# Scores in fewer groups: four blocks of a sliding pair at once, and blocks 2 and 3 of a differential head at once

## The chip, the cores and the metric

The kernel runs on one core of a Trainium2 chip. A core has five engines with queues of their own: TensorE (PE, with its weight loads shown apart as PEld), VectorE (DVE), ScalarE (ACT), GpSimd (POOL) and SyncE (SP), and it has DMA queues. The metric is the device time of one execution in microseconds, lower is better.

## The reference

One decoder layer over 512 tokens of width 1024, batch 1, in fp32. The part around the change is the attention; `h` is the normalised input.

```
qa, ka, va, qd, kd, vd, ga, gd = split(h @ w_in)
# A: sliding window of 128, 8 query heads on 2 key heads of width 64, blocks of 128 queries
scores = qa_block . [previous block, this block of ka] / 8 - slope * distance, outside: -1e30
out_a  = softmax([scores, sink])[..., :-1] @ [previous, this block of va]
# B: differential, 4 heads, each with two maps of width 64 and values of width 128, causal
p      = softmax(qd . kd / 8 - slope * distance), for the two maps
out_d  = rmsnorm((p[0] - lam * p[1]) @ vd) * (1 - 0.2)
merged = sigmoid(ga) * (out_a @ w_branch_swa) + sigmoid(gd) * (out_d @ w_branch_diff)
x      = x + gate1 * (merged @ w_out)
# then a gated MLP with a causal convolution of width 3, and a final norm
```

## The kernel before, in words

Every fp32 product is made from a high and a low part: three matmuls (high by high, high by low, low by high) that add up in one PSUM bank. `mm3` (lines 119 to 121) does so with all 128 rows of the array. In the attention `mm3_rows` (line 126) takes two products at once, each with a contraction of 64, one on rows 0 to 63 and one on rows 64 to 127: the three matmuls of both go out in turns, so that a block of scores for two heads (or two maps) is three pairs of matmuls.

TensorE's order in the attention is written out by hand (`manual_schedule` with TensorE alone): it executes exactly in the order of the program text. VectorE and ScalarE are put in order by a planner, which takes what is ready by its own estimate of time, with priority in the order of the program; operations under `high_priority` (the score reductions, the softmax, the copies of transposes) come before all others, and the rows of the modulation (`arow`, line 757) in part before the rest.

TensorE's gaps are filled with `fill(n)`: n steps, each of three full matmuls of 512 columns that belong to a projection (query, key and value of the differential heads: `pq`, `pk`, `pw`; the gates and branch products of the sliding part: `pga`, `pA`). `fill` also starts the loads of the weights ahead, and every eighth step one piece of the modulation.

The sliding part works on four pairs of heads, `i` = 0 to 3. `swa_scores(i, n0)` makes the scores of two blocks, n0 and n0 + 1, in two PSUM banks; VectorE adds the distances and takes the maxima (line 559, tile `st`). `swa_softmax` has ScalarE take the exponentials and VectorE scale them; `swa_transpose(i, j)` has TensorE transpose the probabilities of one head (line 593, seven transposes, tile `tp`), and ScalarE copies them; `swa_values(i)` (line 604) multiplies them by the values into a bank `oa`, which ScalarE and VectorE copy out (`outah` at line 430, `outal` at line 431). The loop over pairs has this order: scores of blocks 0 and 1 of pair i + 1, two steps, transposes of the first head of pair i, two steps, transposes of the second head, scores of blocks 2 and 3 of pair i + 1, two steps, softmax of pair i + 1, two steps, values of pair i, three steps.

The differential part goes over 16 blocks, s = 4h + n. `diff_scores` makes the scores of a block for two maps (tile `sd`), 128(n + 1) columns wide, and VectorE's reductions follow (line 673); blocks 0 and 1 share a pair of banks and are made together. `diff_softmax` follows, then `diff_transpose` (line 702, tile `td`) and, once a head is done, `diff_values` (tile `od`), whose bank ScalarE empties (lines 719 and 720). In a turn of the loop come two steps, the scores of later blocks, four steps, the transposes of block s, the softmax of the blocks just scored. In the turn of block 1 the scores of block 2 are made, in that of block 2 those of block 3, in that of block 3 those of blocks 0 and 1 of the next head. Some turns have norm sums (`pss`, line 725) or transposes of values (`pv`) between, at fixed counts of steps.

PSUM has eight banks. Here they go by tags: two `f` for projections, three `s` for scores, two `t` for transposes, and one `v` (`vbank`) for the values of both parts and, before, for a projection of the first stage. A tile of a tag waits until the tile before it in that bank has been read.

## Time and profile before

| | us |
|---|---|
| median of 3 runs | 706.9 (706.72 to 707.26) |
| profiled execution | 708.24 |
| span of its instructions | 705.4 |
| TensorE matmuls busy | 685.0 |
| VectorE busy | 578.4 |
| ScalarE busy | 383.9 |

The span is the time from the first to the last instruction; the execution has 2.84 us around it. The mean granted TensorE clock was 0.994 of full speed. Sliding attention lies from about 61 to 117 us, differential attention from 117 to 217 us. In rows in order of time, the first number is the start in us, the second the duration, then engine, line, operation, output and inputs, shapes and the count of instructions merged into the row, and in brackets the idle time before it and what ended it. A matmul's row lasts longer than the distance to the next start, as matmuls overlap.

### The profile page before, as it was taken

What the parts mean: (1) busy time and instruction counts of PE and PEld (TensorE: products, weight loads), DVE (VectorE), ACT (ScalarE), POOL (GpSimd) and SP (SyncE); (2) the same over time, 40 slices, a digit from 0 to 9 for tenths busy, and PEclk for the clock granted to TensorE, in tenths of its full rate; (3) what the DMA queues carried; (4) which work ended last, traced back from release to release, by engine and by line L of the source; (5) the groups of instructions that cost most, each with busy time, mean ns of one, the idle gap of its engine ahead of it and who ended that gap; (6) DMA issues with size and microseconds to landing.
All of it is one profiled execution on the core that took longest, in us unless ns stands there. A gap on an engine that the chain in (4) does not pass through costs nothing. (4 is left out here: it accounts for less than half of the span.)

```text
span 705.4 us, 11197 instructions
## 1 busy us (share of the span) xinstructions
PE 685.0 (97%) x4155; PEld 597.1 (85%) x4155; DVE 578.4 (82%) x1107; ACT 383.9 (54%) x676; POOL 82.2 (12%) x100
## 2 busy tenths in 40 slices
PE   6999999999999999999999999999999999999994
PEld 6777777777787888888889999999999999888884
DVE  5998968788985766773579899888888999979996
ACT  3646766545543333431468656555555666656664
POOL 3000000000011000000030111111101102530300
PEclk9999999999999999999999999999999999999998
DMA  9983624263543774529617888786979748996803
GB/s 311 302 262 98 201 61 154 67 199 90 170 153 100 262 214 142 186 93 288 187 33 148 197 199 204 177 209 182 208 204 230 164 143 204 197 200 191 158 0 119
DMA packets 115861, 121.80 MB, mean 173 GB/s; under 512 B 4415, under 2 KB 93280, under 8 KB 115808
## 3 DMA queue, kind: packets, MB, share of 16 engines
q1 hardware_dynamic: 96894, 95.09, 42.7%
q0 software_dynamic: 18720, 25.73, 21.6%
q8 instruction: 32, 0.52, 0.3%
q10 hardware_dynamic: 194, 0.28, 0.1%
q14 instruction: 21, 0.17, 0.1%
HBM read 118.97 MB, written 2.11 MB: 172 GB/s over the span
## 5 line engine op out<-in xcount | busy, mean ns | idle before, releaser
L1126 PE MATMUL up<-t,m_whi 128*128 128x256 f32 x528 | 96.1, 283 | 0.0
L1126 PEld LDWEIGHTS up<-t,m_whi 128*128 128x128 f32 x528 | 82.3, 192 | 0.0
L1126 PE MATMUL up<-t,m_wlo 128*128 128x256 f32 x264 | 74.7, 283 | 0.1
L1126 PE MATMUL up<-bh,p_wlo 128*128 128x256 f32 x232 | 65.7, 284 | 0.7 <-DVE p_wlo L1069 0.7
L1126 PE MATMUL up<-bh,p_whi 128*128 128x256 f32 x232 | 65.6, 283 | 0.0
L1126 PE MATMUL up<-bl,p_whi 128*128 128x256 f32 x232 | 65.6, 283 | 0.0
L1126 PEld LDWEIGHTS up<-t,m_wlo 128*128 128x128 f32 x264 | 50.6, 192 | 0.3 <-DVE m_wlo L1069 0.3
L1126 PEld LDWEIGHTS up<-bh,p_wlo 128*128 128x128 f32 x232 | 44.5, 192 | 1.1 <-DVE p_wlo L1069 1.1
L1126 PEld LDWEIGHTS up<-bh,p_whi 128*128 128x128 f32 x232 | 44.5, 192 | 0.0
L1126 PEld LDWEIGHTS up<-bl,p_whi 128*128 128x128 f32 x232 | 44.5, 192 | 0.0
L757 DVE SCALAR_TENSOR_TENSOR arow<-ra,cs,arow 128x512 f32<-128x512 f32 x56 | 41.9, 747 | 2.6 <-DMA ra<-in_w_ada_dram 1.8
L1037 POOL DMA_DIRECT2D s<-in_w_up_dram x21 | 27.0, 1361 | 142.9 <-DMA s<-in_w_up_dram 78.0
L1069 DVE TENSOR_TENSOR m_wlo<-s,m_whi 128x1024 fp32r<-128x1024 f32 x31 | 37.7, 1217 | 2.0 <-ACT m_whi L1065 2.0
L1065 ACT CAST m_whi<-s 128x1024 fp32r<-128x1024 f32 x31 | 32.5, 1047 | 9.4 <-DVE s L1059 5.9
L1126 PE MATMUL up<-t,p_whi 128*128 128x256 f32 x176 | 32.2, 283 | 0.0
L687 ACT ACTIVATE sd<-sd,dmx 128x128 f32<-128x128 f32 (+3 forms) x32 | 17.8, 556 | 23.2 <-DVE dmx L685 15.9
L175 POOL TENSOR_TENSOR r<-ms,mhalf 128x1 f32<-128x1 f32 (+1 forms) x16 | 13.2, 828 | 144.7 <-DVE ms L173 74.0
L1126 PEld LDWEIGHTS up<-t,p_whi 128*128 128x128 f32 x176 | 27.4, 192 | 0.2 <-issue 0.2
L1133 ACT ACTIVATE gT<-a,cv 128x512 f32<-128x512 f32 x22 | 17.7, 813 | 17.6 <-DVE a L1168 17.3
L770 POOL DMA_DIRECT2D mod_rows<-arow x8 | 4.3, 540 | 193.7 <-ACT arow L769 193.5
L1065 ACT CAST p_whi<-wa 128x1024 fp32r<-128x1024 f32 x18 | 18.7, 1041 | 12.0 <-PE up L1126 7.2
L1126 PE MATMUL up<-t,p_wlo 128*128 128x256 f32 x88 | 24.9, 283 | 0.0
(478 smaller groups left out, 2073.0 us busy)
## 6 DMA issues: line engine op xcount, KB each, us to landing
ra<-in_w_ada_dram SPq DMA_DIRECT2D x32, 512.0 KB, 4.2
wa<-in_w_up_dram SPq DMA_DIRECT2D x22, 512.0 KB, 4.6
s<-in_w_up_dram SPq DMA_DIRECT2D x21, 512.0 KB, 5.1
s<-in_w_up_dram POOLq DMA_DIRECT2D x21, 512.0 KB, 7.0
adaw<-in_w_ada_dram SPq DMA_DIRECT2D x16, 512.0 KB, 4.9
w<-in_w_in_dram SPq DMA_DIRECT2D x12, 512.0 KB, 4.1
a<-in_w_up_dram SPq DMA_DIRECT2D x11, 512.0 KB, 4.8
b<-in_w_down_dram SPq DMA_DIRECT2D x10, 512.0 KB, 4.7
```

The costliest lines, as they stand in the source:

```text
L175: nc.gpsimd.tensor_tensor(r0, ms, mhalf[:, :n], ALU.pow)
L687: nc.scalar.activation(pm[m], pm[m], AF.Exp, bias=mx[:, m : m + 1], scale=slope, accum_out=lsum[:, m : m + 1])
L757: nc.vector.scalar_tensor_tensor(ac, r[:, a], cc, ac, ALU.mult, ALU.add)
L770: nc.gpsimd.dma_start(mod_rows[idx : idx + 1, hf * S : (hf + 1) * S], row)
L1037: nc.gpsimd.dma_start(dst, upblock(*blk), accum_op=ALU.add)
L1065: nc.scalar.copy(W[J, name][0], R[J, SRC[name]])
L1069: nc.vector.tensor_sub(lo, R[J, SRC[name]], hi.bitcast(F32))
L1126: nc.tensor.matmul(o[u], w[:, k, cu], b[:, k], start=name in ("p1", "m5", "p2") and k == 0 and x == 0, stop=k == 3 and x == 2, skip_group_ ...
L1133: nc.scalar.activation(grow(j), av[J][:, u], AF.Identity, bias=cv[:, 66 + j : 67 + j], scale=cv[:, 44 + j : 45 + j])
```

## The change

`swa_scores` takes a list of blocks. Pair 0 keeps its two calls, (0, 1) and (2, 3). Pairs 1 to 3 have all four blocks made in one call, so that 24 matmuls of 64 rows follow each other; they write four banks, three of tag `s` and, for blocks 2 and 3 of the second head, the one of tag `v`. The call stands behind the first two steps of a turn, directly ahead of the transposes of the first head, and the second call behind the transposes of the second head is gone. All eight reductions of the pair follow the one call.

In the differential part the scores of block 2 and block 3 are made together in the turn of block 1; the turn of block 2 makes none. The second map of block 3 takes the bank of tag `v`. The number of matmuls, reductions and transposes is unchanged, as are the steps of `fill`.

```diff
-    def swa_scores(i, n0):
-        if n0 == 0:
+    def swa_scores(i, blocks):
+        if 0 in blocks:
...
-        sps = [sbank(f"sw{i}_{n0}_{j}", (P, 2, 256)) for j in range(2)]
-        for n in (n0, n0 + 1):
+        sps = {
+            (g, j): vbank(f"sw{i}_{g}_{j}").rearrange("p (a q) -> p a q", a=2)
+            if len(blocks) == NT and (g, j) == (1, 1) else sbank(f"sw{i}_{g}_{j}", (P, 2, 256))
+            for g in sorted({n // 2 for n in blocks}) for j in range(2)
+        }
+        for n in blocks:
...
-                    sps[j][:, n - n0, :w],
+                    sps[n // 2, j][:, n % 2, :w],
...
-        for n in (n0, n0 + 1):
+        for n in blocks:
...
-                        c.sb[n][:, j, :w], sps[j][:, n - n0, :w], dsw[:, 256 - w : 256], 1.0, -3e38, ALU.add, ALU.max,
+                        c.sb[n][:, j, :w], sps[n // 2, j][:, n % 2, :w], dsw[:, 256 - w : 256], 1.0, -3e38, ALU.add, ALU.max,
...
-            sps = [firsts[h][m][:, n, :w] if n < 2 else sbank(f"sd{h}_{n}_{m}")[:, :w] for m in range(2)]
+            sps = [
+                firsts[h][m][:, n, :w] if n < 2 else (vbank if n + m == 4 else sbank)(f"sd{h}_{n}_{m}")[:, :w]
+                for m in range(2)
+            ]
...
-    swa_scores(0, 0)
+    swa_scores(0, (0, 1))
...
-        swa_scores(0, 2)
+        swa_scores(0, (2, 3))
...
+        fill(SWA_FILL[3])
         if more:
-            swa_scores(i + 1, 0)
-        fill(SWA_FILL[3])
+            swa_scores(i + 1, range(NT))
         swa_transpose(i, 0)
         fill(SWA_FILL[4])
         swa_transpose(i, 1)
-        if more:
-            swa_scores(i + 1, 2)
         fill(SWA_FILL[5])
...
-        nxt = {0: (), 1: (s + 1,), 2: (s + 1,), 3: (s + 1, s + 2)}[n] if s < 15 else ()
+        nxt = (s + 1, s + 2) if n % 2 and s < 15 else ()
```

## The prediction, made before the changed kernel was run

> **What bounds the kernel now.** First the page's busy times, then the stretches of attention, then who TensorE waited for there, then its instructions in order of time.

> ```profile
> PE 685.0 (97%) x4155; PEld 597.1 (85%) x4155; DVE 578.4 (82%) x1107; ACT 383.9 (54%) x676; POOL 82.2 (12%) x100
> ```

> The stretch rows below give length, then PE, PEld, DVE, ACT and POOL busy, clock, DMA share and GB/s; the wait rows us, times and the longest.

> ```profile
> 57.00:117.00 60.00, 60.00 (x388) 46.18 (x386) 48.12 (x157) 40.48 (x115) 0.70 (x1) 1.00 0.39 120
> 117.00:217.00 100.00, 97.89 (x523) 77.21 (x523) 86.03 (x232) 52.37 (x121) 5.89 (x6) 1.00 0.47 140
> ...
> PE td L702 <- DVE sd L693: 1.6, 3, 1.1
> PE od L120 <- DVE aTl L431: 0.5, 1, 0.5
> ```

> The reader is to see that TensorE is without a gap in the sliding stage (57 to 117 us) and loses 2.1 us to waits in the differential one (117 to 217), and that VectorE is next at 80% and 86%. From 407 to 591 us TensorE is busy for all 184. So a TensorE saving here should reach the end. Busy includes changes from one kind of matmul to another, which the order of time shows. Transposes alone between full matmuls:

> ```profile
> 97.47 0.39 PE L121 MATMUL pk<-hThA,w_l 128*128 128x512 f32 x1
> 97.70 0.93 PE L593 MATMUL tp<-ident,st 128*128 128x128 f32 x7
> 98.38 0.48 PE L119 MATMUL pk<-hThA,w_h 128*128 128x512 f32 x1
> 98.70 0.40 PE L120 MATMUL pk<-hTlA,w_h 128*128 128x512 f32 x1
> ```

> Transposes with scores behind them:

> ```profile
> 99.62 0.39 PE L121 MATMUL pk<-hThA,w_l 128*128 128x512 f32 x1
> 99.86 0.93 PE L593 MATMUL tp<-ident,st 128*128 128x128 f32 x7
> 100.71 0.97 PE L126 MATMUL sw<-ka,qa 64*128 64x256 f32 x12
> 101.62 0.50 PE L119 MATMUL pk<-hThA,w_h 128*128 128x512 f32 x1
> 101.95 0.39 PE L120 MATMUL pk<-hTlA,w_h 128*128 128x512 f32 x1
> ```

> Block 3 of a differential head by itself:

> ```profile
> 131.04 0.40 PE L121 MATMUL pga<-hThA,wga_l 128*128 128x512 f32 x1
> 131.36 0.96 PE L126 MATMUL sd<-qkv 64*128 64x512 f32 x6
> 132.26 0.50 PE L119 MATMUL pga<-hThA,wga_h 128*128 128x512 f32 x1
> 132.59 0.39 PE L120 MATMUL pga<-hTlA,wga_h 128*128 128x512 f32 x1
> ```

> Full matmuls of 512 columns start 0.23 us apart, a "step". Around scores (64 rows, in pairs) the starts are further apart: 0.32 into the group, 0.33 to 0.34 from the first full matmul behind it to the second. That is what fewer groups can save.

> **The change part by part.** The sum is made against the profiled execution: 708.24 us, a span of 705.4 and 2.84 around it. The median of the runs is 706.9, 1.34 less; a saving is taken off either alike.

> *Differential heads, block 3 joined to block 2, four times.* In head 0, 131.04 to 132.59 is 1.55 us; less two steps (0.46), the group costs 1.09. Its three pairs of 512 columns stream like three full matmuls, 3 x 0.23 = 0.69, and that stays. Saved: 0.40. In heads 1 to 3 the group follows the norm sums (pss): from the start of pss to the second full matmul behind it is 155.03 to 157.13, 2.10 us; the last head's pss, without scores behind it, takes 224.60 to 225.73, 1.13. The group costs 0.97, less 0.69: 0.28 saved. Sum: 0.40 + 3 x 0.28 = 1.24. If the first joined pair's weight load were not hidden (0.11, the 0.34 less the step), it is 0.8; I take 1.24, since that load lies behind a pair of 384 columns.

> *Sliding pairs 1 to 3, two groups into one, three times.* Before, per pair: a group between full matmuls, 68.61 to 70.15, 1.54 - 0.46 = 1.08; transposes alone, 97.47 to 98.70, 1.23 - 0.46 = 0.77; transposes and scores, 99.62 to 101.95, 2.33 - 0.46 = 1.87. Sum 3.72. After: the first group's 1.08; six more pairs at 0.116 each (the 12 weight loads of the group at 100.71 last 0.77, one 0.19, and 0.58 is five pair steps), 0.70; the transposes twice, 1.54; and the change from scores into transposes in place of into a full matmul, which no row shows. That exit costs 0.10 to a full matmul (101.62 to 101.95); into transposes between 0.03 (four transposes that had waited, 0.38 at 164.68 against 0.35) and 0.17 (the way in the other direction, 0.85 against 0.68). I take 0.10, the nearest, which cancels. 3.32; saved 0.40 (0.33 to 0.47), 1.2 in all (1.0 to 1.4).

> The rows make it about 0.4 us for the two changes of a group. [...]

> *Waits that go.* Block 3's transposes waited for VectorE in heads 1 and 3 (0.17 and 0.33 us, of the 1.6 shown). Scored some five microseconds sooner, they find their softmax done: 0.5 saved. The longest, 1.14 us at 144.96, is block 0 of head 1, whose scores, fills and transposes keep their places: kept, with 0 and 2 as ends, since VectorE's order is drawn up anew. The 0.5 before the last head's values stays: there the copy of the transposes is late, whenever they were ready.

> *VectorE and ScalarE.* The same 32 + 32 reductions, exponentials and copies. But a pair's eight reductions come in one burst of 2 x 0.21 + 6 x 0.345 = 2.5 us (starts at 85.95 to 87.06), with the query projection's evacuation behind them: 73.71 to 74.4 now, its bank needed at 77.4, so 1.3 us later is hidden; uncovered, at most 0.5. For block 2 of a head, block 3's two reductions of 0.69 come in front of the softmax and TensorE arrives 0.3 to 0.4 sooner. The softmax was ready 3.72, 2.96, 1.35 and 3.5 us before the transposes; 1.95, 1.3, -0.3 and 1.85 are left. In head 2, however, one of the two is already in front (182.28, the result at 183.5), so that margin is still 0.4: cost 0, end 0.3.

> *SP and POOL.* The score functions issue no DMA, and the two fills that now come first keep their loads in the same order. Cost 0.

> *The values' bank as fourth: the added wait.* A merged sliding group writes it in its second half. For pair 2 it must first be emptied of pair 0's values, whose second copy is VectorE's (outal):

> ```profile
> 81.11 1.54 DVE L757 SCALAR_TENSOR_TENSOR arow<-ra,cs,arow 128x512 f32<-128x512 f32 x2 [0.70 <-DMA ra<-in_w_ada_dram]
> ...
> 87.06 0.68 DVE L431 TENSOR_TENSOR outal<-oa,outah 128x512 fp32r<-128x512 f32 x1
> ```

> It ends at 87.74. Now nobody asks before 91.39. After, the group starts at 81.82 + 0.23 - 0.40 + six steps (1.38) + 0.09 = 83.1, and needs the bank some 0.8 us later, at 83.9. Pair 1's exponentials come about 3 us sooner, so VectorE may do the copy sooner, but its work up to there is the same: 87.74 less the 0.70 idle at 81.11 and the 1.11 us of four pair-2 reductions (85.95 to 87.06), which now come later, is 85.9; if the two modulation rows at 81.11 (1.46 us) fall behind the copy too, 84.5. Wait: 0.6 to 2.0, and as no row says whether they do, the middle, 1.3. The outer ends are 0 and the 3.8 of today's order. Behind the waiting matmul stand the whole TensorE queue, the next transposes first, and for those ScalarE's copies. For pair 3 the copy ends at 97.41 now, 6.0 us after the values began; the bank is needed 6.2 us after, with 2 us of idle on VectorE before it: 0. Pair 1 finds the bank empty since 67.3. In the heads ScalarE empties it 1.3 us after the values, and block 3 comes over 3 us after them: 0.

> *Sum.* -1.24 - 1.2 - 0.5 + 1.3 = -1.64: 706.9 - 1.6 = **705.3 us**; the profiled execution 706.6, span 703.8.

> **The rivals.**

> *The bank is free in time.* Everything but the wait: -2.94, 704.0 us. For it: the copy needs only ScalarE's half before it, and the softmax of pair 1 is earlier. Against: VectorE is busy 9.1 of 10 us from 75 to 85.

> *The values' bank comes late (the other side).* If the copy stays behind pair 2's first four reductions, it ends at 87.74 and the wait is 3.8: +0.9, 707.8 us; with the weight split of 1.22 in front of it as well, 5.0: +2.1, 709.0. It decides from 2.94 us of wait on, an end of the copy past 86.8. For it: today's order is exactly that; against: the group now comes two fills later. [...] In the trace of before no score group waits for a bank.

> *Softmax for two blocks queues up.* If block 3's exponentials and products (2 us) also go in front of block 2's, the margins above become about -0.05, -0.7, -2.3 and -0.15, 3.2 us of waits: +1.5, 708.4. It decides from 1.7 on. For it: VectorE's 86%; against: block 2 is first in the program's order.

> *All waits go,* the 1.14 too: -4.1, 702.8 us.

> **How the numbers follow.** 0.2% (1.4 us: 705.5 and 708.3) is about what a measurement here can tell from no change. Chances: forecast 0.42 (own range 704.3 to 706.2; 0.26 of it below 705.5); bank in time 0.22; bank late 0.16 (half of it above 708.3); queueing softmax 0.12 (half and half); all waits gone 0.08. Faster: 0.26 + 0.22 + 0.08 = 0.56. Same: 0.16 + 0.08 + 0.06 = 0.30. Slower: 0.08 + 0.06 = 0.14. The range 703.0 to 708.0 leaves out most of the last case (0.07) and the upper halves of two (0.12).

> **What would show it.** Seven score groups fewer; sw groups of 24 matmuls for pairs 1 to 3, sd groups of 12 throughout; each 0.3 to 0.4 us shorter than its two forerunners; no waits before four-block transposes; one wait at the fourth bank, named sw behind outal (L431 now), of 0.6 to 2.0. The forecast is wrong if that wait is over 3 or absent, if transposes wait more than today's 1.6 us in sum, or if TensorE finishes attention earlier and a later wait takes it back.

## The result and the profile after

The changed kernel takes 716.62 us (716.24 to 719.72), the kernel before beside it 706.81 (706.55 to 707.26): a ratio of 1.0141, 95% interval 1.0123 to 1.0158, so 1.4% slower. The forecast was 705.3 us, 0.2% faster, with a range from 703.0 to 708.0.

The page of the changed kernel has the same matmuls and the same busy time in a longer span:

```profile
span 714.9 us, 11187 instructions
PE 684.8 (96%) x4155; PEld 598.5 (84%) x4155; DVE 577.1 (81%) x1107; ACT 383.7 (54%) x676; POOL 81.1 (11%) x100
```

The stretch rows of the two attention parts, with the columns of before (length, then PE, PEld, DVE, ACT and POOL busy, clock, DMA share, GB/s); the second ends at 227 us since the part now does. Behind them the wait rows for the same time:

```profile
57.00:117.00 60.00, 56.26 (x355) 44.24 (x354) 44.19 (x149) 37.88 (x110) 0.70 (x1) 0.97 0.36 110
117.00:227.00 110.00, 102.28 (x550) 81.26 (x549) 88.29 (x237) 54.56 (x125) 4.93 (x6) 0.98 0.46 136
```

```profile
PE td L709 <- DVE sd L700: 5.6, 2, 2.8
PE sw L126 <- DVE outal L431: 2.6, 1, 2.6
PE od L120 <- DVE aTl L431: 1.2, 1, 1.2
PE pv L641 <- ACT pT L599: 1.1, 1, 1.1
PE td L709 <- DVE dls L697: 0.6, 1, 0.6
PE od L119 <- ACT aTh L430: 0.3, 1, 0.3
```

The reader is to see two things. TensorE waits 11.4 us where it waited 2.1 us before (the sums of the wait rows). And the clock of both parts, 1.00 before, is now 0.97 and 0.98: something ran at a lower clock behind the waits.

What was forecast of the groups is there. Pair 3's group of 24 matmuls, which meets no wait (pair 1's, from 69.88 to 72.85, is as long):

```profile
99.81 0.39 PE L121 MATMUL pk<-hThA,w_l 128*128 128x512 f32 x1
100.12 1.67 PE L126 MATMUL sw<-ka,qa 64*128 64x128 f32 x24
101.73 0.98 PE L597 MATMUL tp<-ident,st 128*128 128x128 f32 x7
102.47 0.48 PE L119 MATMUL pk<-hThA,w_h 128*128 128x512 f32 x1
102.78 0.39 PE L120 MATMUL pk<-hTlA,w_h 128*128 128x512 f32 x1
```

From 99.81 to 102.78 it is 2.97 us, less two steps of 0.23 is 2.51; with the second head's transposes (0.77) 3.28 against 3.72 before: 0.44 saved, where 0.40 was forecast.

To see where the time went, the span is cut at the first score matmul of the sliding part (sw), the first of the heads (sd), the first matmul of the second gates (pgd) and of the output (oc); the output ends at the first matmul of the MLP (up). The lengths are differences of these starts:

| us | sliding | heads | gates | output |
|---|---|---|---|---|
| before | 55.3 | 135.4 | 66.5 | 46.3 |
| after | 59.7 | 141.4 | 66.5 | 45.4 |

All of the loss, 10.4 us, is in the two attention parts. The span grows by 9.5 us only, since the output takes some 0.8 us less: a wait of 0.65 us that the profiled execution of before has there (`th` for `xn`) is absent. The next paragraphs follow the four pauses of the attention parts that are new or over 1 us longer than before (2.61, 2.75, 2.84 and 1.13 us), and the clock.

**The fourth bank.** VectorE's instructions in order of time, while TensorE's second half of pair 2's scores stood from 83.96 to 86.57 (TensorE's row behind them):

```profile
82.77 0.75 DVE L764 SCALAR_TENSOR_TENSOR arow<-ra,cs,arow 128x512 f32<-128x512 f32 x1 [0.34 <-DMA ra<-in_w_ada_dram]
83.43 0.68 DVE L431 TENSOR_TENSOR qkv<-pk,qkv 128x512 fp32r<-128x512 f32 x1
84.03 0.74 DVE L764 SCALAR_TENSOR_TENSOR arow<-ra,cs,arow 128x512 f32<-128x512 f32 x1
84.69 1.22 DVE L116 TENSOR_TENSOR w_l<-w,w_h 128x1024 fp32r<-128x1024 f32 x1
85.83 0.68 DVE L431 TENSOR_TENSOR outal<-oa,outah 128x512 fp32r<-128x512 f32 x1
...
86.57 1.35 PE L126 MATMUL sw<-ka,qa 64*128 64x256 f32 x11 [2.61 <-DVE outal L431]
87.85 1.75 PE L597 MATMUL tp<-ident,st 128*128 128x128 f32 x7
89.26 0.77 PE L119 MATMUL pw<-hThB,w_h 128*128 128x512 f32 x1
```

The copy `outal` stands behind two rows of the modulation, the keys' copy (`qkv`) and a weight split of 1.22 us. It starts at 85.83. The bank is needed at 83.96, as worked out (83.9). And behind the wait the seven transposes take 1.75 us in place of 0.98, a full matmul 0.77 in place of 0.48: the clock row below has 0.51 there.

**Block 0 of head 1** (TensorE waits 2.75 us, to 151.26). VectorE:

```profile
141.47 0.56 DVE L431 TENSOR_TENSOR aTl<-td,aTh 128x384 fp32r<-128x384 f32 x1
145.21 0.49 DVE L762 TENSOR_SCALAR arow<-ra,cs 128x512 f32<-128x512 f32 x1 [3.19 <-DMA mod_rows<-arow]
145.61 0.28 DVE L680 CUSTOM_DVE_ANT_0 sd<-sd,ddf 128x128 f32<-128x128 f32 x1
```

The block's first reduction (145.61) stands behind a modulation product that overwrites `arow`, and that product waits 3.19 us until the row before has been stored. In the kernel before, too, the product stands ahead of the reductions, but nothing waits there:

```profile
138.93 0.48 DVE L755 TENSOR_SCALAR arow<-ra,cs 128x512 f32<-128x512 f32 x1
139.32 0.28 DVE L673 CUSTOM_DVE_ANT_0 sd<-sd,ddf 128x128 f32<-128x128 f32 x1
```

There the store was issued at 136.74 and took 1.6 us, and VectorE came to the product at 138.93. Now it is issued at 141.37, VectorE comes to the product at 142.0, and the 2 KB take 3.8 us; SyncE issued a load of 512 KB at 141.40. The store follows TensorE's sum of the row (`pr`) by 2.3 us in both kernels. VectorE came to the product 4.5 us behind that sum before and comes 2.9 us behind it now, as block 3's products of head 0, which lay in between (135.92 to 137.2), come sooner now (138.08 to 139.3).

**Block 2 of head 1** (TensorE waits 2.84 us, to 170.26). ScalarE's exponentials, then VectorE's products:

```profile
162.12 0.62 ACT L694 ACTIVATE sd<-sd,dmx 128x384 f32<-128x384 f32 x1 [3.59 <-DVE dmx L692]
162.73 0.71 ACT L694 ACTIVATE sd<-sd,dmx 128x512 f32<-128x512 f32 x1
163.69 0.72 ACT L694 ACTIVATE sd<-sd,dmx 128x512 f32<-128x512 f32 x1
164.41 0.60 ACT L694 ACTIVATE sd<-sd,dmx 128x384 f32<-128x384 f32 x1
...
166.18 0.48 DVE L699 TENSOR_SCALAR sd<-sd,dls 128x512 f32<-128x512 f32 x1
166.71 0.74 DVE L700 SCALAR_TENSOR_TENSOR sd<-sd,dls,sd 128x512 f32<-128x512 f32 x1
168.04 0.41 DVE L699 TENSOR_SCALAR sd<-sd,dls 128x384 f32<-128x384 f32 x1
168.37 1.22 DVE L116 TENSOR_TENSOR w_l<-w,w_h 128x1024 fp32r<-128x1024 f32 x1
169.50 0.61 DVE L700 SCALAR_TENSOR_TENSOR sd<-sd,dls,sd 128x384 f32<-128x384 f32 x1
```

Block 2 is the one with 384 columns. Its maxima were taken by 159.6, but the small operation behind them (`dmx`, line 692), for which its first exponential waits, comes at 161.86, behind a weight split and block 3's reductions. Both exponentials of block 3 (512) lie ahead of its second one, both products of block 3 ahead of its own, and a weight split between its two products.

**The value transposes in the sliding part** (1.13 us, `pv`). They wait for ScalarE's copy of the second head's transposed probabilities. The copy in the kernel before, then copy and `pv` now:

```profile
100.55 0.97 ACT L595 COPY pT<-tp 128x512 f32<-128x512 f32 x2 [1.13 <-PE tp L593]
...
106.08 0.94 ACT L599 COPY pT<-tp 128x512 f32<-128x512 f32 x2
106.70 0.66 PE L641 MATMUL pv<-ident,vT 128*128 128x128 f32 x4 [1.13 <-ACT pT L599]
```

TensorE made the transposes from 103.94 on, but ScalarE took 105.00 to 106.08 for pair 3's first exponentials, and copied from 106.08. Before, the copy began 0.69 us after the transposes (99.86), pair 3's second scores lay on TensorE between them and `pv`, and its exponentials came from 103.53 on.

**The clock.** Stretches of about 3.4 us of the changed kernel, same columns; the seventh is the clock. The first pair lies around the pause at the fourth bank, the second around block 0, the three rows after that around block 2:

```profile
83.50:87.00 3.50, 0.89 (x13) 0.69 (x13) 3.50 (x6) 0.62 (x1) 0.00 (x0) 0.99 0.28 54
87.00:90.40 3.40, 3.40 (x19) 2.98 (x16) 2.87 (x19) 1.07 (x2) 0.00 (x0) 0.51 0.79 254
...
148.40:151.80 3.40, 0.65 (x4) 0.52 (x4) 3.40 (x12) 1.00 (x5) 0.00 (x0) 1.00 0.63 170
151.80:155.20 3.40, 3.40 (x13) 3.12 (x13) 3.36 (x6) 0.54 (x2) 0.00 (x0) 0.50 0.60 196
...
165.50:168.90 3.40, 1.92 (x9) 1.24 (x7) 3.00 (x11) 1.03 (x2) 0.37 (x1) 1.00 0.00 0
168.90:172.30 3.40, 2.04 (x13) 1.53 (x13) 1.77 (x3) 0.48 (x1) 0.00 (x0) 1.00 0.43 119
172.30:175.70 3.40, 3.40 (x26) 2.82 (x25) 1.57 (x11) 1.25 (x2) 0.00 (x0) 1.00 0.12 42
```

With the prices of the next section the loss adds up. Sliding: pauses 2.61 + 1.13, half clock 1.6, three groups at -0.44: 4.0 of the 4.4. Heads: pauses 7.7 against 2.1, half clock 1.6, groups -1.2: 6.0 of the 6.0.

### The profile page after: what moved, and what is told of

Same layout as the page of the kernel before. It is cut to its first block, busy times and chain, and to the rows that moved or that the text cites. A ratio compares the mean times of both kernels' runs of the same rounds, so it can differ in the third digit from the quotient of the medians.

```text
span 714.9 us, 11187 instructions
## 1 busy us (share of the span) xinstructions
PE 684.8 (96%) x4155; PEld 598.5 (84%) x4155; DVE 577.1 (81%) x1107; ACT 383.7 (54%) x676; POOL 81.1 (11%) x100
```

## The experiments

**Each half of the change alone.** The sliding pairs changed and the heads as before (these lines against the changed kernel), then the kernel before with these lines the other way round:

```diff
-            sps = [
-                firsts[h][m][:, n, :w] if n < 2 else (vbank if n + m == 4 else sbank)(f"sd{h}_{n}_{m}")[:, :w]
-                for m in range(2)
-            ]
+            sps = [firsts[h][m][:, n, :w] if n < 2 else sbank(f"sd{h}_{n}_{m}")[:, :w] for m in range(2)]
...
-        nxt = (s + 1, s + 2) if n % 2 and s < 15 else ()
+        nxt = {0: (), 1: (s + 1,), 2: (s + 1,), 3: (s + 1, s + 2)}[n] if s < 15 else ()
```

> The sliding half of the change alone; the differential part as before. Theory (waits and the clock after them): saves 3 x 0.44 us of group changes, but keeps the wait for the values' bank (2.6 us), 1.7 us of half clock behind it and the 1.1 us wait of the value transposes: about +4 us, 710.9. Rival (the sliding half is what was forecast, and the loss is all in the differential part): 705 to 706.

> The differential half alone; the sliding part as before. Theory: saves 1.2 us of group changes and 0.5 of waits, but block 2 of head 1 waits about 2.8 us for a softmax that stands behind block 3's, and block 0 of head 1 some 1.6 us more with 1.7 us of half clock behind it: about +4.5 us, 711.3. Rival (the loss is all in the sliding part, whose late end upsets the heads): 705 to 706. If the two halves are independent, both differences add up to 9.8.

Measured: 712.66 us for the sliding pairs alone (ratio 1.0075, 1.0047 to 1.0104) and 712.12 for the heads alone (1.0070, 1.0043 to 1.0097), beside 707.41 for the kernel before in the same series. 5.3 and 4.7 us make 10.0, the whole change 9.8: as far as the intervals tell, the halves lose independently. In the first, the heads' part takes 135.7 us, as before, and the sliding part 60.8; in the second, the sliding part is untouched (55.3), the heads take 140.6. What the sliding groups displace does not make the heads late, and the other way round.

**The values' copies first.** VectorE and ScalarE take the copy out of the values' bank ahead of rows and splits:

```diff
-        evac(outa[0][:, i], outa[1][:, i], o)
+        with tc.high_priority(offset=HP):
+            evac(outa[0][:, i], outa[1][:, i], o)
```

> The whole change, but the copies of the values out of their bank have the priority of the score reductions. Theory: the 2.6 us wait at the fourth bank goes and with it the 1.7 us of half clock behind it: 716.6 - 4.3 = 712.3. Rival (the wait is for TensorE's own earlier work or for the bank's readers in general, not for where the copy stands on VectorE): 716 to 717.

Measured: 711.28 us (1.0058, 1.0041 to 1.0074), 5.3 less than the changed kernel. No pause at the fourth bank, the sliding part 55.2 us, no half clock behind it. The wait was one of order on VectorE, as its rows say. With it gone, the 1.12 us pause at `pv` still stands, and the groups about pay for it. The heads are 2.2 us shorter as well (139.2), though the edit does not touch them: the pause at block 0 of head 1 is 2.57 us here, with no half clock behind it, and the wait of 0.6 us at head 0 is absent.

**Warm through the wait.** Twelve matmuls ahead of pair 2's block 2 keep TensorE busy while the fourth bank is not free:

```diff
         for n in blocks:
+            if i == 2 and n == 2:
+                for _ in range(12):
+                    nc.tensor.matmul(sps[1, 0][:, 0, :P], ident, ones, start=True, stop=True)
```

> The whole change, with twelve 128-column fp32 matmuls on the identity put ahead of block 2 of pair 2, into a bank that block 2 then overwrites: TensorE is busy while it would wait for the fourth bank. Theory (a pause of 2.6 us is what halves the granted clock after it): no half clock at 87 us, 1.7 us gained, 714.9. Rival (the half clock comes from something else): 716.6 or more, with half clock at 87 us still there.

Measured: 715.98 us (1.0118, 1.0082 to 1.0153), against 716.62; the two intervals overlap, so the total alone decides little. The profile does:

```profile
83.50:87.00 3.50, 3.50 (x36) 3.25 (x36) 3.50 (x11) 0.62 (x1) 0.00 (x0) 1.00 0.53 155
87.00:90.40 3.40, 3.40 (x23) 3.01 (x24) 1.75 (x12) 2.65 (x9) 0.00 (x0) 1.00 0.53 154
```

The second half of the scores starts 3.76 us after the first (82.22 to 85.98), where it was 3.68 (82.89 to 86.57): the bank comes no sooner. But TensorE is busy, and the clock behind it stays at 1.00. From there to the second head's transposes it is 3.11 us (85.98 to 89.09) where it was 4.68 (86.57 to 91.25): the half clock cost 1.57 us, and the idle time, not the bank, brought it.

**Block 3's softmax one turn later.** The scores of block 3 stay with block 2's on TensorE; its reductions, exponentials and products are issued where they were before:

```diff
         for s, sps, w in ops:
+            parts3[s] = sps, w
+            if s % NT != 3:
+                diff_reduce(s)
+
+    parts3 = {}
+
+    def diff_reduce(s):
+        for sps, w in (parts3[s],):
...
         if nxt:
             diff_scores(*nxt)
+        if n == 1:
+            nxt = (s + 1,)
+        elif n == 2:
+            nxt = (s + 1,)
+            diff_reduce(s + 1)
```

> The changed kernel, in which block 3's scores still stand at once with block 2's on TensorE, but block 3's maxima and exponentials (reductions, exponentials, products) are issued one turn later, as in the kernel before. Theory (block 2 of a head waits since VectorE gets block 3's products ahead of its own): of the three long pauses of the changed kernel, the third, 2.84 us ahead of block 2's transposes of head 1, goes; no half clock lay behind it, so the time is 716.6 - 2.8 = 713.8 us, and the heads' stage falls from 141.4 to 138.6 us. The pause at block 0 of head 1 (2.75 us) and that at the fourth bank (2.61 us) stay. Rival (block 2's scores themselves come too late, since a group of twelve takes longer than one of six): the pause stays above 2 us and the time at 716 to 717 us.

Measured: 712.99 us (1.0073, 1.0051 to 1.0095), 3.6 less; 2.8 were expected. The heads' part is 138.1 us (138.6 expected). The sliding part, which the edit does not touch, is 2.0 us shorter too (57.7): the pause at the fourth bank is 2.17 us here, and no half clock follows it. The longest waits of TensorE in its attention, and VectorE in order of time at head 1's blocks 2 and 3:

```profile
PE td L717 <- DVE sd L708: 2.6, 1, 2.6
PE sw L126 <- DVE outal L431: 2.2, 1, 2.2
```

```profile
160.97 0.42 DVE L707 TENSOR_SCALAR sd<-sd,dls 128x384 f32<-128x384 f32 x1
161.43 0.62 DVE L708 SCALAR_TENSOR_TENSOR sd<-sd,dls,sd 128x384 f32<-128x384 f32 x1
...
163.12 0.49 DVE L707 TENSOR_SCALAR sd<-sd,dls 128x512 f32<-128x512 f32 x1
```

Block 2's products (384) come first again, and one long `td` wait is left of two (2.6 us, block 0). The scores were not late; the softmax was.

**The modulation product behind block 1.** The first product of the row that waits for the store is moved, and the row's loads start two units later:

```diff
             for hf in range(2):
...
+                if (idx, hf) == (1, 0):
+                    yield
+                    yield
...
-                                nc.vector.tensor_scalar_mul(ac, r[:, a], cc)
+                                with tc.issue_after(mixed[5].ins) if (idx, hf) == (1, 0) else ExitStack():
+                                    nc.vector.tensor_scalar_mul(ac, r[:, a], cc)
```

`mixed[5]` is the last softmax product of block 1 of head 1, and each `yield` lets eight steps pass.

> The changed kernel, with the first product of the second adaptation row (the one that waits for the store of the row before it, 3.19 us of VectorE) placed behind block 1's products of head 1 instead of ahead of block 0's reductions; its loads start two units later. Theory (block 0 of head 1 waits for a store that VectorE waits for): the pause of 2.75 us at block 0 of head 1 goes or falls to some 1 us, and with it the half clock behind it (3.4 us at half, 1.7 us): 716.6 - 2.75 - 1.7 = 712.2 us. If the half clock has another cause than the pause, it stays at 151 to 155 us and the time is 713.9. As VectorE's order behind the moved product shifts too (block 2's products come ahead of block 3's here), the pause at block 2 may go with it: then 709.3 us. Rival (the merged groups make block 0 late by themselves): the pause stays and the time is 716 to 717 us.

Measured: 715.28 us (1.0100, 1.0068 to 1.0132). The mechanism shows: the heads' part is 135.3 us, 6.1 less than in the changed kernel, neither 2.75 nor 2.84 is left (block 2's products now come ahead of block 3's), and there is no half clock at 150 us. But the time falls by 1.3 us only, not by 4 to 7, since the gates' part goes from 66.5 to 69.8 us and the output's from 45.4 to 47.1. With the two units of delay one more modulation row falls into the gates' part (three sums of rows on TensorE there, two before), and TensorE waits 1.6 us there for weight splits.

**All four pauses taken away.** The values' copies first, block 3's softmax later, the product behind block 1, and pair 3's exponentials behind the last copy of pair 2's transposes:

```diff
-                nc.scalar.copy(pt[:, b * 512 : b * 512 + wb], tp[:, :wb])
+                c.turned = nc.scalar.copy(pt[:, b * 512 : b * 512 + wb], tp[:, :wb])
...
     def swa_softmax(i):
-        with tc.high_priority(offset=HP):
+        with tc.high_priority(offset=HP), tc.issue_after(pairs[2].turned.ins) if i == 3 else ExitStack():
```

> The changed kernel with its four new waits taken away at once: the copies of the sliding values ahead of VectorE's and ScalarE's other work (fourth bank, 2.61 us), the copies of the second head's transposed probabilities of the third pair ahead of the next pair's exponentials (1.13 us), the first product of the second adaptation row behind block 1's products (2.75 us) and block 3's maxima and exponentials one turn later (2.84 us). Theory (the groups save what was forecast, 2.4 us, and the four waits with the half clock behind two of them take 9.2 + 3.4 us): 716.6 - 9.2 - 3.4 = 704.0 us, 2.8 under the kernel before, if no pause of over 2 us and so no half clock is left. Rival (fewer groups bring nothing by themselves, or the waits come back elsewhere): 706.8 us or more.

> The kernel before, its groups as they were, with three of the four remedies that its code has room for: the sliding values' copies first, the second head's copies of the third pair ahead of the next exponentials, and the first product of the second adaptation row behind block 1's products. Theory (the remedies only take away waits that the merged groups made): within 0.5 us of 706.8; at most 1.1 us less, if the one wait of the kernel before at block 0 of head 1 (1.14 us) goes with the moved product. Rival (what the remedied changed kernel gains over the kernel before comes from the remedies, not from the groups): as low as that kernel, 704 to 705 us.

Measured: 709.94 us (1.0031, 1.0018 to 1.0044) for the changed groups, where 704.0 was expected. The two attention parts do come to 187.8 us, 2.9 under the kernel before (some 0.5 of it since two matmuls of a modulation row now fall into the gates), but the gates lose 3.4 and the output 1.1, much as in the run before. Three of the remedies, those for which the kernel before has room, give there 717.07 us (1.0134, 1.0108 to 1.0160), not within 0.5 of it: its heads lose 2.6 us (two new `td` waits of 1.3 and 1.9 us), its gates 4.3, with a stretch of half clock at 285.7 us. So my expectation of "no effect" was wrong: VectorE's order carries such a move through the rest of the kernel. What it does show is that these remedies bring the kernel before no gain.

**The rows catch up.** As all four, but the moved row and the next give the two units back:

```diff
-                    yield
+                    if (idx, hf, k) not in ((1, 0, 4), (1, 1, 2)):
+                        yield
```

> The changed kernel with the same four remedies, but the adaptation rows behind the moved one catch up its two units, so that the later rows and the weights that share their buffers come when they did in the kernel before. Theory (the four waits gone, the groups save 2.9 us of the two attention stages, and the 3.3 us that the gates' stage and 1 to 2 us that the output's stage lost with the four remedies came from the rows' later loads): attention 187.8 us, gates 66.5, output 45.4, in all 703.5 to 704.5 us, some 2.9 below the kernel before. Rival (the gates lose their time to the groups or to the moved maxima, not to the rows): the gates' stage stays at 69 to 70 us and the time at 707 to 710 us.

Measured: 707.06 us (0.9994, 0.9979 to 1.0008). The gates are back at 66.5 us and the output at 45.4, so the loss there was the rows' delay. But head 2's block scores now wait 1.6 us for the keys (`sd` behind `qkv`, line 431), whose copy stands on VectorE behind eight row products from 176.7 to 185.6 us, and a stretch of half clock follows: the heads' part is 136.1 us, and the total no better than before. That the row products are the cause was not tested by itself.

**The sliding pairs alone, with their two remedies,** and the same remedies in the kernel before:

> Only the sliding pairs changed (groups of four blocks, the values' bank as fourth), the heads' groups as before, with the two remedies of the sliding stage: the values' copies first, and the second head's copies of the third pair ahead of the next exponentials. Theory: the sliding stage falls from 55.3 to 53.9 us, the heads' stage stays near 135.5: 1.2 to 1.5 us under the kernel before, 705.4 to 705.7 where that is 706.8. Rival (fewer groups in the sliding pairs bring nothing, the remedied waits were all there was): the sliding stage at 55.2 us and the time as before.

> The kernel before with the same two remedies of the sliding stage, and its groups as they were. Theory (the remedies alone bring nothing, since neither wait is there): the sliding stage at 55.2 to 55.3 us and the time within 0.4 us of the kernel before. Rival (the remedies themselves bring the gain): 1.2 us or more below it.

Measured: 706.90 us (0.9994, 0.9981 to 1.0007) and 707.26 (0.9998, 0.9989 to 1.0007). In the profiled execution the sliding part is 53.9 us, 1.5 less, as expected, its heads 135.7 and its span 703.0 against 705.4. But this execution is the fastest of the twelve, whose spans go up to 707.2; their median is 704.5, against 705.0 for the kernel before in the same series. The median time shows 0.2 us, with an interval from 1.3 less to 0.5 more. What takes the rest back in the other executions no trace here shows; it stays open. In the kernel before the remedies are without effect.

**The order alone.** All four remedies, but the modulation's loads stay in their places. The product that waits for the store is issued one `yield` later and behind the reductions of blocks 0 and 1:

```diff
+                    if (idx, hf, k) == (1, 0, 0):
+                        yield
...
+                                with tc.issue_after(mixed[5].ins) if (idx, hf) == (1, 0) else ExitStack():
+                                    nc.vector.tensor_scalar_mul(ac, r[:, a], cc)
...
-                    yield
+                    if (idx, hf, k) != (1, 0, 0):
+                        yield
...
-                    nc.vector.tensor_tensor_reduce(
+                    mixed[s] = nc.vector.tensor_tensor_reduce(
```

> The changed kernel with all four remedies, where the product that waits for the adaptation row's store comes behind the reductions of blocks 0 and 1 of head 1 and one step later, while all loads stay in their places. Theory (the waits cost what they measured, the later loads made the losses of the two versions before): the attention stages at 188 to 189 us, gates 66.5, output 45.4, a profiled span of 702 to 703.5 us; the median, which in the sliding pairs alone fell by only 0.2 us where the stage fell by 1.5, between 704.3 and 706 us against 706.8 to 707.1 before. Rival (each remedy brings a new wait elsewhere, as a wait for the queries came in head 2 of the version that caught up): a pause of over 1.5 us in a head, and a median within 0.5 us of the kernel before or above it.

Measured: **705.20 us** (703.34 to 706.67) against 707.48, a ratio of 0.9959, 0.9945 to 0.9974: 0.4% faster than the kernel before, and by the two ratios 1.8% faster than the change as made. Its attention, by stretch rows and then by TensorE's waits there:

```profile
57.00:117.00 60.00, 60.00 (x400) 47.20 (x398) 48.98 (x159) 41.75 (x116) 0.70 (x1) 1.00 0.40 123
117.00:214.00 97.00, 94.24 (x507) 75.56 (x503) 84.31 (x232) 51.90 (x120) 5.67 (x6) 1.00 0.49 147
```

```profile
PE td L718 <- DVE sd L709: 1.6, 1, 1.6
...
PE od L120 <- DVE aTl L431: 0.9, 1, 0.9
...
PE od L119 <- ACT aTh L430: 0.3, 1, 0.3
```

TensorE is without a gap in the sliding part, the clock is 1.00 in both parts, and the gates (66.5) and the output (45.6; 45.4 in the changed kernel) keep their time. The two attention parts are 188.2 us, 2.6 under the kernel before although they wait 2.8 us and not 2.1. So TensorE saves 3.2 us outside these waits; by the starts of its matmuls, some 2.7 of them lie at the groups' changes. One sign of the rival is there all the same, the pause of 1.56 us at block 0 of head 1. The moved product alone, with the loads in their places, was not tried in the kernel before. The store takes 3.8 us here too, but VectorE meets it behind the reductions and waits 0.82 us for it, not 3.19.

## Why the prediction was wrong

The sign was wrong, and one of the prediction's own signs of being wrong came: transposes wait 6.2 us in sum where it allowed 1.6. Point by point:

- *Groups, -1.24 and -1.2: right.* Where no wait disturbs, head 0's joined block 3 saves 0.41 us (125.09 to 127.16 in the last kernel, 2.07 less two steps, against 0.93 and 1.09 before), head 1 saves 0.27, a sliding pair 0.44. Sum 2.5; the forecast was 2.44.
- *Waits that go, -0.5: right, and given back.* The 0.17 and 0.33 us are gone, but the wait of the last head's values (`od`) rose from 0.5 to 1.4, and one of 0.6 came at head 0's block 0.
- *"1.14 us at block 0 of head 1: kept, with 0 and 2 as ends": mis-sized, and outside its ends.* It was 2.75 us. The step looked at scores, fills and transposes, all unmoved, and not at what stands ahead of the block's reductions on VectorE. There was a product whose release is a store of 2 KB, 0.6 us to spare before. The store came to 0.6 us ahead of VectorE, not 2.2, and took 3.8 us, not 1.6. "SP and POOL: cost 0" is the same miss: the number and order of DMAs was right, their times against each other were not.
- *Block 2's softmax, "cost 0, end 0.3": this step failed.* It was 2.84 us in head 1, and nothing in the other heads. The margins of 1.95, 1.3, 0.4 and 1.85 were counted with block 3's reductions ahead only. The rival "softmax for two blocks queues up" had the mechanism, with 3.2 us over all four heads, most of it in head 2 (2.5 in sum, if head 2 starts from the margin of 0.4 that the step before had found). It was given 0.12 because "block 2 is first in the program's order". On VectorE and ScalarE that order does not decide in this kernel: a planner takes what it thinks is ready, and put block 3's exponentials and products ahead. The run with block 3's softmax later removed the wait.
- *The fourth bank, +1.3 (0.6 to 2.0): mis-sized.* It was 2.61 us. The bank was asked for at 83.96 (forecast 83.9); the copy began at 85.83 and ended at 86.5 (forecast 84.5 to 85.9). The four reductions did leave, and nothing else came in: apart from them, VectorE's operations up to the copy are the same as before. But of the 0.70 us idle, which the step took off as well, 0.59 stayed: 0.25 for ScalarE at 80.94 and 0.34 for a modulation row's load at 82.77. That is the 0.6 us over the upper end. The two modulation rows at the lower end stayed ahead of the copy. The wait is short of the 2.94 from which the late rival decides.
- *The value transposes, 1.13 us: not seen at all.* The scores between transposes and `pv` had covered ScalarE's copies. A step that takes a group away from a place has to ask what it covered there; this one counted only what was bought by taking it.
- *The clock, 1.6 us twice: not priced.* Every pause was costed at its own length. The pause of 2.61 us at the fourth bank cost 4.2 with the 1.57 of half clock behind it.
- *The chances.* The upper halves of the two rivals make 0.14, as under "Slower", not the 0.12 of the sentence on the range.

Sum: the pauses came to 9.3 us more than before, the clock to 3.1, the groups to -2.5: +9.9, of the 10.4 measured in the two attention parts, against the forecast -1.64 for the whole. The causes of the fourth bank's and of block 2's pause were shown each by itself, and `pv`'s by two runs that differ in the sliding part by its remedy alone (55.2 us with the values' copies first, 53.9 with both). Block 0's went in a run in which block 2's went too, and its half clock was not tested apart.

## What to carry to other kernels

Joining groups on the engine that bounds saved here what the rows show of the changes between kinds of matmul, 0.27 to 0.44 us a group and 2.5 us in all; the same edit moves each group's consumers, so price for every engine behind it what now stands ahead of the first thing that TensorE waits for, by name, whichever order the program has. Ask too what the group had covered at the place it leaves. And where a remedy is found, move only the one instruction in its queue: moving its loads along cost 5.0 us in the gates and the output here, where the wait was 2.75.

## What the hardware showed that was not expected

**Half clock behind a pause, by stretches of 3.41 us.** If the boundaries of the clock records are continued in steps of 3.413 us, the idle time of TensorE within one stretch can be set against the clock of the next. For stretches at full clock in the attention and gate parts of all the kernels here:

| idle in the stretch, us | clock in the next 3.41 us |
|---|---|
| 2.17, 2.47, 2.61, 2.61, 2.67, 2.75 | half, 6 of 6 |
| 1.83, 1.63, 1.60 | half |
| 1.84, 1.67 | full |
| 1.5 and less | full, all of them |

Once at half, the clock was full again after one stretch, but in the kernel with the sliding pairs alone only after two, though TensorE idled 0.36 us of the first. So a pause of 2.84 to 2.88 us, split by an end of a stretch, brought no half clock in four kernels. A pause of 2.17 us at the fourth bank shows both: whole in one stretch (the kernel with the modulation product behind block 1) it brought half clock and a sliding part of 59.3 us, split (the kernel with block 3's softmax later) it brought none and 57.7 us, 1.6 less. The same kernel's times spread wider with such pauses in it (709.5 to 715.3 us for the one with block 3's softmax later, where the kernel before has 706.3 to 709.8). The clock goes with it: the kernel with the heads alone took 710.19 us at a mean clock of 0.997 and 714.39 at 0.988, with its four other runs in order between. That the clock differs by where the stretches lie, which would change from run to run, is an argument and was not shown. The step of 3.413 us is that of the clock records of the changed kernel and the one before: the half stretches that end within the span are 3.413 us long, and the full stretches between half ones are 20, 18 and 162 times that in the changed kernel and 200 times in the one before. None of the stretches ahead of half clock in the table was idle throughout; TensorE worked for 0.65 to 1.8 us of them.

**A small store beside a large load.** The store of 2 KB that block 0 of head 1 depends on took 1.6 us in the five kernels here where the next 512 KB load was issued 2.3 us after it, and 3.6 to 3.8 us in the nine where it was issued 0.03 us after. Of all the stores of modulation rows in these traces, the 18 with such a load up to 0.05 us behind took 2.6 to 4.7 us, while most others took 1.5 to 1.9. Some others took up to 3.7 us, so the load is not the only cause, and that it is one was not tested by an edit. No run here shows what a store's time is made of.
